# A two-layer decoder trunk on one core: own slots for half of the value weights, the gate scaled into SBUF, a pad 64 bytes wider

## The chip, the cores and the metric

The kernel runs on one core of a Trainium2 chip. What counts is the device time of one execution in microseconds (us), lower being better; the time of a kernel is the median of its runs. A core has five engines that work side by side and each run their own list of instructions in order: TensorE (PE in the profile, its weight loads PEld), VectorE (DVE), ScalarE (ACT), GpSimd (POOL) and SyncE (SP), whose work here is to issue DMA transfers. SBUF is the working memory; PSUM holds the results of TensorE. Semaphores order the engines among each other.

## The reference

1024 tokens of width 1024 pass two residual layers and a last RMS norm. Layer 1 is a gated linear recurrence, layer 2 is attention with a forget gate:

```python
def fox_mixer(h, w_in, b_f, w_out):
    u = h @ w_in
    q, k, v, gate = ...            # 16 heads of 64 each, from the columns of u
    f_logit = u[..., 4 * FOX_WIDTH:] + b_f
    cum = jnp.cumsum(jax.nn.log_sigmoid(f_logit), axis=1)
    logits = (q . k) * scale + (cum_q - cum_k)      # causal
    p = jax.nn.softmax(logits, axis=-1)
    y = (p @ v) * jax.nn.silu(gate)
    return y @ w_out

for i in range(2):
    x = x + (lru_mixer, fox_mixer)[i](rms_norm(x, norm_g[i]), ...)
return rms_norm(x, final_g)
```

All inputs and the output are float32.

## The kernel before

**Products.** A float32 product is made of three matmuls in a faster format: both factors are split into a high part (the value rounded to that format) and a low part (the rest), and high x high, low x high and high x low are added up in PSUM. The activations' parts are called `hh` and `hl`, those of weights `wh` and `wl`. A weight pack of 128x512 numbers is split in three steps by `split_weights`: a DMA brings it into a buffer `wf` (three buffers in all), ScalarE casts it to `wh`, and VectorE (GpSimd in some places) subtracts to get `wl`. The `wh` and `wl` of all weights of layer 2 (query, key, gate, value, output) share four slots each in the pool `wpool`.

**Layer 1** takes the first 440 us or so, layer 2 the rest. The change concerns layer 2, but for the pad.

**Layer 2.** Heads go in pairs. For each head and each half of its 512 queries, `maxima` makes the logits `S` (TensorE), their maximum (VectorE, L702) and the exponentials `p` (ScalarE, L707), 128 queries at a time; `weigh` turns `p` by transposes into PSUM (`pt`), splits it into `ph` and `pl` (ScalarE and VectorE) and multiplies with the values (`O`). In between, as filling for TensorE, `kq_units` makes the next pair's queries and keys, `g_units` its gate, both through `project`, and `values` the values of two pairs at a time.

`project` makes, for each half of the tokens, a product of 24 matmuls in one of two PSUM banks of the tag `g`, multiplies it in place by the row `rs1` of reciprocal RMS values (VectorE, L511), and hands it to `use`. For the gate, `use` is tanh on ScalarE from the PSUM bank into `sg` in SBUF (L672), and then on VectorE (tanh + 1) x gate (L673; the operation is a scalar_tensor_tensor, STT for short), which reads `sg` and the PSUM bank. The bank is free after that.

`values(g)` for g = 1 to 3 is taken up in the heads 3, 7 and 11 (at some 620 to 656, 763 to 800 and 908 to 943 us). It has four weight packs (k = 0, 2, 4, 6). The first two are split before the generator's first `yield`, the third and fourth (k = 4 and 6) after it. They take slots of `wpool`: the first two those that the queries' weights leave, the others those that the gate's weights leave. Then come eight tiles `vps` of 24 matmuls of 128x256, in turn in the two banks `g`; each is split into the values `v` by ScalarE and VectorE (L546).

**What sets the order.** The text of the program gives only a first order: `run` takes steps from the generators as a string of digits and dots says. The framework's scheduler then simulates the program and orders each engine's instructions by it, and gives buffers to tiles in the order in which they come free in that simulation. Each engine runs its list in order, so an instruction that waits holds up all behind it on that engine; the DMA issues on SP's queue likewise.

**Placement.** Pools lie on the left or the right side of SBUF. `pad2` lies on the left, ahead of `hT` (the pool of `hh` and `hl`), `w` (`wpool`), and all left-side pools of both layers. On the right side lie, among others, `rs`, the recurrence's temporaries with the `xch`, `xcl`, `wgh` and `wgl` that layer 1's `gate` products read, and in layer 2 the values, the queries and keys, and `rs1`.

Of the kernel before, what the change touches and what calls it, by code (L numbers as in the profile page):

```python
# [11 lines left out]
F32 = mybir.dt.float32  # L12
F32R = mybir.dt.float32r
BF16 = mybir.dt.bfloat16
AF = mybir.ActivationFunctionType
ALU = mybir.AluOpType

P = 128
SEQ = 1024
HALF = 512  # L20
KT = 8
# [12 lines left out]
def f32(ap):  # L34
    return ap.bitcast(F32)
# [3 lines left out]
def trunk(ctx: ExitStack, tc: tile.TileContext, xt, w0, wg, wo0, pc, gn, gf, w1, wv, wf, bf, wo1, out):  # L39
    nc = tc.nc  # L40

    def pool(name, bufs, **kw):
        return tc.tile_pool(name=name, bufs=bufs, **kw)
# [2 lines left out]
    const.tile([P, 32], F32, name="pad0")  # L46
    ctx.enter_context(pool("edge", 1, side="right")).tile([P, 56], F32, name="pad1")
    dram = ctx.enter_context(pool("dram", 1, space=DRAM))
    ctx.enter_context(pool("gap", 1)).tile([P, 24], F32, name="pad2")
    hpool = ctx.enter_context(pool("hT", 16))  # L50
    wpool = ctx.enter_context(pool("w", 4))
    ps = ctx.enter_context(pool("ps", 2, space=PSUM))
# [3 lines left out]
    def matmul(*args, **kw):  # L56
        pe[0] = nc.tensor.matmul(*args, **kw)  # L57
        return pe[0]
# [26 lines left out]
    def to_hi(hi, src, eng, scale=None):  # L85
        if eng is nc.scalar:
            if scale is None:
                nc.scalar.copy(hi, src)  # L88
            else:
                nc.scalar.activation(hi, src, AF.Copy, scale=scale)  # L90
        elif eng is nc.gpsimd:
            nc.gpsimd.tensor_scalar(hi, src, 1.0 if scale is None else scale, 0.0, ALU.mult, ALU.add)
        elif scale is None:
            eng.tensor_copy(hi, src)
        else:
            eng.tensor_scalar(hi, src, scale, None, ALU.mult)

    def to_lo(lo, src, hi, eng):
        return eng.tensor_tensor(lo, src, f32(hi), ALU.subtract)  # L99

    def split_weights(src, shape, hi_eng, lo_eng, parts=wpool):
        n = shape[0] * shape[1]
        room = -(-n // 64) * 64
        a = wpool.tile([P, room], F32, tag="wf", name="wf", bufs=3)[:, :n]
        b = parts.tile([P, room], F32R, tag="wh", name="wh")[:, :n]
        c = parts.tile([P, room], F32R, tag="wl", name="wl")[:, :n]
        wt, hi, lo = (t.rearrange("p (a b) -> p a b", a=shape[0]) for t in (a, b, c))
        for part, sl in src:
            nc.sync.dma_start(wt[:, :, sl], part)
        to_hi(b, a, hi_eng)  # L110
        to_lo(c, a, b, lo_eng)
        return [(hi[:, k], lo[:, k]) for k in range(shape[0])]
# [66 lines left out]
    late = ctx.enter_context(ExitStack())  # L179
    with ExitStack() as l0:  # L180
# [42 lines left out]
        k = 0  # L223
# [84 lines left out]
        def silu(s, gps, parts=(slice(0, SEQ),)):  # L308
            gs = gps.rearrange("p a b -> p (a b)")
            sg = s["sg"] = long("sg")  # L310
            for cs in parts:
                g_, s_ = gs[:, cs], sg[:, cs]
                nc.vector.tensor_tensor(g_, g_, rs[:, cs], ALU.mult)
                nc.scalar.activation(s_, g_, AF.Tanh, scale=0.5)
                nc.vector.scalar_tensor_tensor(s_, s_, 1.0, g_, ALU.add, ALU.mult)
                yield
# [22 lines left out]
        def outputs(n, parts=(slice(0, SEQ),), gate=itertools.repeat(None)):  # L339
            s = state.pop(n)  # L340
            y = tuple(ypool.tile([P, SEQ], F32R, tag=z, name=z) for z in ("yh", "yl"))
            for cs, _ in zip(parts, gate):
                a_ = s["a"][:, cs]
                nc.vector.tensor_tensor(a_, a_, s["sg"][:, cs], ALU.mult)
                yh, yl = (z[:, cs] for z in y)
                to_hi(yh, a_, nc.scalar)
                to_lo(yl, a_, yh, nc.vector)
            ys.append(y)
# [86 lines left out]
        recur(NB - 1, halves)  # L435
        outputs(NB - 1, halves, silu(state[NB - 1], gps, halves))
        lru.close()
        vpool = late.enter_context(pool("v", 1, side="right"))
        kqpool = late.enter_context(pool("kq", 1, side="right"))
        rpool = late.enter_context(pool("R", 2, side="right"))  # L440
# [4 lines left out]
        rs1 = [rpool.tile([P, HALF], F32, tag="R", name="rs1") for h in range(2)]  # L445
# [9 lines left out]
        for h, cs in enumerate(halves):  # L455
            y = [tuple(z[:, cs] for z in p) for p in ys[-2:]]
            hT[h] = [pair() for k in range(KT)]
            parts = split_x(h, 1)
# [29 lines left out]
    with ExitStack() as l1:  # L488
        tu = l1.enter_context(pool("tu", 1))
        at = l1.enter_context(pool("at", 2))  # L490
# [15 lines left out]
        def project(w, use, hs=(0, 1)):  # L506

            for h in hs:
                pt = ps.tile([P, HALF], F32, tag="g", name="gps1")
                yield from gemm_steps(pt, zip(w, hT[h]))  # L510
                nc.vector.tensor_tensor(pt, pt, rs1[h], ALU.mult)  # L511
                use(h, pt)

        def values(g):

            ex = HEADS if g == 0 else 0
            parts = []
            for k in range(0, KT, 2):
                src = [(wv[g, :, k : k + 2], slice(0, 256))]
                if ex:  # L520
                    src.append((wf[:, k : k + 2], slice(256, 256 + ex)))
                parts += split_weights(src, (2, 256 + ex), nc.scalar, nc.gpsimd if ex else nc.vector)
                if k == 2:
                    yield
            Vs[2 * g], Vs[2 * g + 1] = [], []
            for st in range(8):
                if ex and st % 2:
                    pt = ps.tile([P, SEQ], F32, tag="S", name="vps")[:, : 256 + ex]
                else:
                    pt = ps.tile([P, 256 + ex], F32, tag="g", name="vps")  # L530
                c = (st % 4) * P
                for k in range(KT):
                    xh, xl = hT[st // 4][k]
                    wh, wl = parts[k]
                    xh, xl = xh[:, c : c + P], xl[:, c : c + P]
                    matmul(pt, xh, wh, start=k == 0, stop=False)
                    matmul(pt, xl, wh, start=False, stop=False)
                    matmul(pt, xh, wl, start=False, stop=k == KT - 1)
                    if k % 4 == 1:
                        yield  # L540
                r_ = rms1[st // 4][:, st % 4 : st % 4 + 1]
                for a in range(2):
                    v = vpool.tile([P, 4, HD], F32R, tag=f"v{st}", name=f"v{st}", bufs=2)
                    src = pt[:, a * P : (a + 1) * P].rearrange("p (b d) -> p b d", b=2)
                    to_hi(v[:, 0::3], src, nc.scalar, scale=r_)
                    nc.vector.scalar_tensor_tensor(v[:, 1:3], src, r_, f32(v[:, 0::3]), ALU.mult, ALU.subtract)  # L546
                    Vs[2 * g + a].append(v)
                if ex:
                    nc.vector.tensor_scalar(fz[:, st], pt[:, 256:], r_, None, ALU.mult)
# [10 lines left out]
        def low(pair):  # L560
            return nc.vector if pair else nc.gpsimd

        def kq_units(pair, parts=((1, (0, 1)), (0, (0, 1)))):

            for is_k, hs in parts:
                if hs[0] == 0:
                    kq[pair, is_k] = tuple(
                        kqpool.tile([P, SEQ], F32R, tag=f"qk{p}{is_k}", name=f"qk{p}") for p in "hl"
                    )
                if hs[0] == 0 or pair == 0:  # L570
                    kqw[is_k] = list(weights(w1[is_k * 8 + pair], lo_eng=low(pair)))
                hi, lo = kq[pair, is_k]
                eng = nc.vector if pair == 0 else nc.scalar

                def use(h, pt):
                    cs = halves[h]
                    if is_k:
                        to_hi(hi[:, cs], pt, eng)
                        to_lo(lo[:, cs], pt, hi[:, cs], nc.vector)
                    else:  # L580
                        to_hi(hi[:, cs], pt, eng, scale=0.125)
                        nc.vector.scalar_tensor_tensor(lo[:, cs], pt, 0.125, f32(hi[:, cs]), ALU.mult, ALU.subtract)  # L582

                yield from project(kqw[is_k], use, hs)
# [78 lines left out]
        def g_units(pair, hs=(0, 1)):  # L663

            if hs[0] == 0:
                sgs[pair] = at.tile([P, SEQ], F32, tag="sg", name="sg1")
                gw[0] = list(weights(w1[16 + pair], lo_eng=low(pair)))
            sg = sgs[pair]

            def use(h, pt):  # L670
                g_ = sg[:, h * HALF : (h + 1) * HALF]
                nc.scalar.activation(g_, pt, AF.Tanh, scale=0.5)  # L672
                nc.vector.scalar_tensor_tensor(g_, g_, 1.0, pt, ALU.add, ALU.mult)  # L673

            yield from project(gw[0], use, hs)

# [294 lines left out]
        for hd in range(HEADS):  # L971
# [29 lines left out]
            side = late() if hd == 14 else iter(())  # L1001
# [99 lines left out]
```

## Time and profile before

| | |
|---|---|
| runs | 1130.3, 1131.4 and 1128.25 us, median 1130.3 |
| the profiled execution | 1132.74 us |
| its span, first to last instruction | 1130.9 us, so 1.8 us lie around it |
| mean granted clock of TensorE | 0.995 |
| busy in the span | TensorE 98%, VectorE 67%, ScalarE 52%, GpSimd 15% |
| moved by DMA | 105.43 MB, mean 93 GB/s |

Rows of a timeline give the start in us from the span's start, the duration in us, the engine, the line of the kernel, the operation and its operands (output<-inputs by the program's names, buffer numbers left out), the shapes, and in brackets how long the engine sat idle before, and for what. In grouped rows stand the count, the busy time in us, the mean in ns of one, and the idle time before them. Matmuls are pipelined, so the pace of TensorE is read from one start to the next, not from durations.

### The profile page before, as it was taken

Reading aid. Unit: us, or ns where it says so; the run is one execution under the profiler, and the core shown is the slowest. Engines: PE = TensorE matmul, PEld = TensorE weight load, DVE = VectorE, ACT = ScalarE, POOL = GpSimd, SP = SyncE. Lnnn points to the kernel's source line nnn. Section 1 sums busy time; section 2 is a strip of 40 time slices with the busy share of each in tenths; the row PEclk is TensorE's granted clock in tenths of the full one; section 3 lists DMA queues with packets and bytes.
Section 4 is the critical chain, followed back from the end, with each engine's and each line's share of the span. In section 5 each row is a group of like instructions: output and inputs, shape, how many; then the busy total and the mean of one; then the engine's idle time right before and its main releaser. Section 6 shows DMA issues by size and latency. Waiting matters only on the chain.

```text
span 1130.9 us, 15754 instructions
## 1 busy us (share of the span) xinstructions
PE 1112.0 (98%) x5681; PEld 937.3 (83%) x5681; DVE 762.2 (67%) x1271; ACT 589.6 (52%) x1077; POOL 165.6 (15%) x105
## 2 busy tenths in 40 slices
PE   9999999999999999999999999999999999999997
PEld 7786888888888887988888888888888888878886
DVE  7789756876568789666676466763666645676645
ACT  8387445354453666455555355553555534554435
POOL 1312112121121202330110100101001010010110
PEclk9999999999999999999999999999999999999999
DMA  6111121111211114443334124252142421665445
GB/s 216 52 42 52 43 61 38 52 52 42 61 37 52 56 57 144 124 123 103 99 89 119 52 84 109 75 123 62 58 120 85 110 81 52 182 180 157 151 149 186
DMA packets 63702, 105.43 MB, mean 93 GB/s; under 512 B 9508, under 2 KB 24484, under 8 KB 63624
## 3 DMA queue, kind: packets, MB, share of 16 engines
q1 hardware_dynamic: 63624, 104.42, 31.3%
q8 instruction: 45, 0.74, 0.3%
q14 instruction: 33, 0.27, 0.1%
HBM read 63.30 MB, written 15.93 MB: 70 GB/s over the span
## 4 chain that ended last, share of the span: by engine, by line
PE 87%; DVE 4%; ACT 2%; DMA 2%; issue 2%; POOL 1%; SPq 0%; POOLq 0%; ACTq 0%
PE gps L57 32%; PE ops L57 15%; PE ups L57 10%; PE vps L57 7%; PE S L57 6%; PE O L57 6%; PE pt L61 5%; PE turn L57 3%; PE gate L57 2%; POOL wl L99 1%; DMA wf<-in_w 1%; DVE sq L167 1%; ACT wh L88 1%; DVE x L470 0%; DMA x<-in_xt 0%
## 5 line engine op out<-in xcount | busy, mean ns | idle before, releaser
L57 PE MATMUL gps<-hh,wh 128*128 128x512 f32 x576 | 228.6, 397 | 1.0 <-DVE qkl L582 1.0
L57 PE MATMUL gps<-hl,wh 128*128 128x512 f32 x576 | 226.0, 392 | 0.0
L57 PE MATMUL gps<-hh,wl 128*128 128x512 f32 x576 | 226.0, 392 | 0.0
L88 ACT CAST wh<-wf 128x512 fp32r<-128x512 f32 (+2 forms) x156 | 94.6, 607 | 146.6 <-PE gps L57 49.2
L707 ACT ACTIVATE p<-S,m 128x128 f32<-128x128 f32 (+7 forms) x128 | 94.9, 741 | 135.2 <-DVE m L702 134.1
L99 POOL TENSOR_TENSOR wl<-wf,wh 128x512 fp32r<-128x512 f32 (+1 forms) x60 | 100.7, 1685 | 389.4 <-ACT wh L88 332.5
L99 DVE TENSOR_TENSOR pl<-pt,ph 128x512 fp32r<-128x512 f32 (+1 forms) x198 | 98.8, 540 | 81.7 <-ACT ph L88 81.3
L57 PEld LDWEIGHTS gps<-hl,wh 128*128 128x128 f32 x576 | 108.4, 188 | 23.8
L57 PEld LDWEIGHTS gps<-hh,wh 128*128 128x128 f32 x576 | 108.6, 189 | 20.2 <-DVE qkl L582 1.2
L57 PEld LDWEIGHTS gps<-hh,wl 128*128 128x128 f32 x576 | 108.9, 189 | 19.7 <-POOL wl L99 0.7
L702 DVE CUSTOM_DVE_ANT_0 S<-S,mask 128x128 f32<-128x128 f32 (+7 forms) x128 | 97.3, 761 | 30.2 <-PE S L57 25.8
L734 POOL TENSOR_TENSOR sg<-sg,recb 64x1024 f32<-64x1024 f32 (+1 forms) x17 | 38.8, 2282 | 460.8 <-DMA recb<-recd 400.8
L88 ACT CAST ph<-pt 128x512 fp32r<-128x512 f32 (+1 forms) x198 | 83.6, 473 | 30.6 <-PE pt L61 25.3
L57 PE MATMUL S<-T,U 96*128 96x512 f32 (+7 forms) x384 | 91.7, 348 | 2.4 <-ACT p L707 2.4
L99 DVE TENSOR_TENSOR wl<-wf,wh 128x512 fp32r<-128x512 f32 x96 | 70.0, 733 | 26.5 <-ACT wh L88 25.8
L369 DVE TENSOR_TENSOR x<-x,ops 128x512 f32<-128x512 f32 x80 | 54.1, 682 | 48.1 <-PE ops L57 48.1
L57 PEld LDWEIGHTS S<-T,U 128*128 128x128 f32 (+1 forms) x384 | 68.3, 189 | 15.6 <-ACT p L707 3.6
L61 PE MATMUL pt<-ident,p 128*128 128x128 f32 x576 | 79.4, 273 | 0.0
L57 PE MATMUL ups<-hh,wh 128*128 128x512 f32 x192 | 76.6, 400 | 1.7 <-ACT hh L90 1.0
L61 PEld LDWEIGHTS pt<-ident,p 128*128 128x128 f32 x576 | 67.4, 141 | 12.4 <-issue 2.2
L57 PE MATMUL vps<-wh,hh 128*128 128x256 f32 (+1 forms) x256 | 74.6, 292 | 3.0 <-DVE sg L673 2.1
L57 PE MATMUL ups<-hh,wl 128*128 128x512 f32 x192 | 76.0, 396 | 1.5 <-POOL wl L99 1.5
(176 smaller groups left out, 2260.0 us busy)
## 6 DMA issues: line engine op xcount, KB each, us to landing
wf<-in_w SPq DMA_DIRECT2D x100, 256.0 KB
wf<-in_wo SPq DMA_DIRECT2D x64, 128.0 KB
U<-qkh SPq DMA_DIRECT2D x64, 128.0 KB
T<-qkh SPq DMA_DIRECT2D x28, 256.0 KB
x<-in_xt SPq DMA_DIRECT2D x16, 256.0 KB
x1d<-x SPq DMA_DIRECT2D x16, 256.0 KB
wf<-in_wv SPq DMA_DIRECT2D x16, 256.0 KB
U<-qkl SPq DMA_DIRECT2D x32, 128.0 KB
```

The costliest lines, as they stand in the source:

```text
L57: pe[0] = nc.tensor.matmul(*args, **kw)
L61: pe[0] = nc.tensor.transpose(*args)
L88: nc.scalar.copy(hi, src)
L99: return eng.tensor_tensor(lo, src, f32(hi), ALU.subtract)
L167: eng.tensor_tensor(parts[0], parts[0], sq, ALU.add)
L369: nc.vector.tensor_tensor(x, x, pt, ALU.add)
L702: nc.vector.tensor_tensor_reduce(S[:, :n], S[:, :n], mask[:, SEQ - n :], -1.0, -NEG, ALU.add, ALU.min, accum_out=m)
L707: seen[0] = nc.scalar.activation(p, S[:, :n], AF.Exp, bias=m, scale=-1.0, accum_out=sums[:, i : i + 1])
L734: nc.gpsimd.tensor_tensor(sg, sg, recs[hd // 2][rows, cs], ALU.mult)
```

## The change

Three things are changed.

1. A new pool `vw` on the right side has two slots each for `wh` and `wl`. The third and fourth weight packs of `values(1)` to `values(3)` take them, and the generator yields only after all four packs are split.
2. The scaling by `rs1` moves from `project` into each `use`. For queries and keys it is the same instruction at the same place. For the gate it now writes to `sg` in SBUF, the tanh reads `sg` and writes a new tile `t1` (in the buffers of the tag `xp`), and the STT works on `t1` and `sg`. The number of instructions is the same.
3. `pad2` is 40 instead of 24 numbers wide, so that everything behind it on the left side moves by 64 bytes, from 192 to 0 modulo 256.

```diff
-    ctx.enter_context(pool("gap", 1)).tile([P, 24], F32, name="pad2")
+    ctx.enter_context(pool("gap", 1)).tile([P, 40], F32, name="pad2")
...
+        vwpool = late.enter_context(pool("vw", 2, side="right"))
         vpool = late.enter_context(pool("v", 1, side="right"))
...
                 pt = ps.tile([P, HALF], F32, tag="g", name="gps1")
                 yield from gemm_steps(pt, zip(w, hT[h]))
-                nc.vector.tensor_tensor(pt, pt, rs1[h], ALU.mult)
                 use(h, pt)
...
-                parts += split_weights(src, (2, 256 + ex), nc.scalar, nc.gpsimd if ex else nc.vector)
-                if k == 2:
+                parts += split_weights(
+                    src, (2, 256 + ex), nc.scalar, nc.gpsimd if ex else nc.vector, wpool if ex or k < 4 else vwpool
+                )
+                if k == (2 if ex else KT - 2):
                     yield
...
                 def use(h, pt):
                     cs = halves[h]
+                    nc.vector.tensor_tensor(pt, pt, rs1[h], ALU.mult)
...
                 g_ = sg[:, h * HALF : (h + 1) * HALF]
-                nc.scalar.activation(g_, pt, AF.Tanh, scale=0.5)
-                nc.vector.scalar_tensor_tensor(g_, g_, 1.0, pt, ALU.add, ALU.mult)
+                nc.vector.tensor_tensor(g_, pt, rs1[h], ALU.mult)
+                t = at.tile([P, HALF], F32, tag="xp", name="t1", bufs=2)
+                nc.scalar.activation(t, g_, AF.Tanh, scale=0.5)
+                nc.vector.scalar_tensor_tensor(g_, t, 1.0, g_, ALU.add, ALU.mult)
```

The scheduler moves instructions at the three `values` stages. The first stage serves as the example. On TensorE, the end of the gate's second half (`gps1`) and the start of the value tiles: before, the first tile's last pack (`wh_5480`) stands behind the gate and the four `O` products, and the second tile begins after it.

```order
L57 MATMUL gps1_5387<-hl_3438,wh_5255 128x512
L57 MATMUL O_5326<-ph_5444,v6_3962 128x256
L57 MATMUL O_5326<-pl_5445,v6_3962 128x256
L57 MATMUL O_5326<-ph_5447,v7_3994 128x128
L57 MATMUL O_5326<-pl_5448,v7_3994 128x128
L57 MATMUL vps_5485<-wh_5480,hh_3295 128x256
L57 MATMUL vps_5485<-wh_5480,hl_3296 128x256
L57 MATMUL vps_5485<-wl_5481,hh_3295 128x256
L57 MATMUL vps_5485<-wh_5480,hh_3297 128x256
L57 MATMUL vps_5485<-wh_5480,hl_3298 128x256
L57 MATMUL vps_5485<-wl_5481,hh_3297 128x256
L57 MATMUL vps_5516<-wh_5307,hh_3283 128x256
```

After the change the second tile (`vps_5525`) follows the `O` products at once:

```order
L57 MATMUL gps1_5407<-hl_3441,wh_5262 128x512
L57 MATMUL O_5345<-ph_5464,v6_3965 128x256
L57 MATMUL O_5345<-pl_5465,v6_3965 128x256
L57 MATMUL O_5345<-ph_5467,v7_3997 128x128
L57 MATMUL O_5345<-pl_5468,v7_3997 128x128
L57 MATMUL vps_5525<-wh_5314,hh_3286 128x256
```

The first tile (`vps_5494`) now ends ahead of the gate's last six matmuls: its last six are done ahead of the transposes `pt_5440` of before (`pt_5460` now).

On VectorE, at the same place, before: the scaling in PSUM, the low part of the fourth pack, the sum of `yo`, the STT of the gate, and then the first value tile.

```order
L99 TENSOR_TENSOR pl_5448<-pt_5440,ph_5447 128x128
L511 TENSOR_TENSOR gps1_5387<-gps1_5387,rs1_3254 128x512
L99 TENSOR_TENSOR wl_5481<-wf_5479,wh_5480 128x512
L780 TENSOR_TENSOR yo_4994<-yo_4994,O_5326 64x512
L673 SCALAR_TENSOR_TENSOR sg1_5247<-sg1_5247,gps1_5387 128x512
L546 SCALAR_TENSOR_TENSOR v0_5510<-vps_5485,rms10_3251,v0_5510 128x128
```

And after, where the two operations on the first value tile stand ahead of the scaling, and the low part is that of the next pair's weights:

```order
L548 SCALAR_TENSOR_TENSOR v0_5519<-vps_5494,rms10_3254,v0_5519 128x128
L99 TENSOR_TENSOR pl_5465<-pt_5460,ph_5464 128x256
L99 TENSOR_TENSOR pl_5468<-pt_5460,ph_5467 128x128
L548 SCALAR_TENSOR_TENSOR v0_5522<-vps_5494,rms10_3254,v0_5522 128x128
L675 TENSOR_TENSOR sg1_5254<-gps1_5407,rs1_3257 128x512
L99 TENSOR_TENSOR wl_5773<-wf_5771,wh_5772 128x512
L785 TENSOR_TENSOR yo_5001<-yo_5001,O_5345 64x512
L678 SCALAR_TENSOR_TENSOR sg1_5254<-t1_5491,sg1_5254 128x512
```

On SP's queue, half a head earlier, the loads of the third and fourth packs. Before, the third (`wf_5473`) stands ahead of the T loads and the fourth (`wf_5479`) behind the U loads:

```order
L109 DMA wf_5473<-in_wv 128x512
L591 DMA T0_3575<-qkh_4854 64x1024
L592 DMA T0_3575<-qkh_4854 64x1024
L593 DMA T0_3575<-qkl_4855 64x1024
L605 DMA U_3577<-cumd_3567 2x512
L602 DMA U_3577<-qkh_5056 64x512
L603 DMA U_3577<-qkh_5056 64x512
L604 DMA U_3577<-qkl_5057 64x512
L109 DMA wf_5479<-in_wv 128x512
```

After, the fourth (`wf_5331`) stands right behind the T loads, and two loads of the next pair's key weights (`in_w1`) take places among the U loads:

```order
L109 DMA wf_5325<-in_wv 128x512
L594 DMA T0_3578<-qkh_4861 64x1024
L595 DMA T0_3578<-qkh_4861 64x1024
L596 DMA T0_3578<-qkl_4862 64x1024
L109 DMA wf_5331<-in_wv 128x512
L608 DMA U_3580<-cumd_3570 2x512
L109 DMA wf_5765<-in_w1 128x512
L605 DMA U_3580<-qkh_5063 64x512
L606 DMA U_3580<-qkh_5063 64x512
L607 DMA U_3580<-qkl_5064 64x512
L109 DMA wf_5771<-in_w1 128x512
```

On ScalarE the casts of the third and fourth packs move from the head's second half into the half before, to places directly ahead of the exponentials `p` of 384 and of 512 columns, and two casts of the next pair's key weights take the places they leave.

## The prediction

> **What bounds the kernel now.** I read the page's first part, the waits of TensorE, the timeline around the longest recurring ones, and then the rows of what they wait for.
>
> ```profile
> PE 1112.0 (98%) x5681; PEld 937.3 (83%) x5681; DVE 762.2 (67%) x1271; ACT 589.6 (52%) x1077; POOL 165.6 (15%) x105
> ```
>
> ```profile
> PE vps L57 <- DVE sg L673: 2.1, 3, 0.7
> ...
> PE vps L57 <- ACT wh L88: 0.9, 3, 0.3
> PE vps L57 <- DVE wl L99: 0.7, 3, 0.2
> ```
>
> TensorE is the bound: it is busy 98% of the span, and of the engines that feed it none passes 67%. Three of its waits belong to `vps` (the value projection), come three times each and are what this change touches (columns: us in all, times, longest). The first of the three stages, on TensorE:
>
> ```profile
> 631.43 0.39 PE L57 MATMUL gps<-hl,wh 128*128 128x512 f32 x1
> ...
> 631.96 0.27 PE L57 MATMUL O<-pl,v 128*128 128x128 f32 x1
> 632.53 0.39 PE L57 MATMUL vps<-wh,hh 128*128 128x256 f32 x1 [0.30 <-ACT wh L88]
> ...
> 633.26 0.39 PE L57 MATMUL vps<-wl,hh 128*128 128x256 f32 x1 [0.22 <-DVE wl L99]
> 633.48 0.28 PE L57 MATMUL vps<-wh,hh 128*128 128x256 f32 x1
> 633.60 0.28 PE L57 MATMUL vps<-wh,hl 128*128 128x256 f32 x1
> ...
> 634.70 0.39 PE L57 MATMUL vps<-wh,hh 128*128 128x256 f32 x1 [0.70 <-DVE sg L673]
> ```
>
> A running `vps` matmul starts 0.12 us after the one before (633.48, 633.60); the first after a wait takes 0.22 (633.26 to 633.48). From 631.96 to 634.70 are 2.74 us; one 128-wide `O` (0.06, half of a 256-wide one) and six `vps` would need 0.78. With the slow start at 634.70 (0.10) the stage loses 2.06 us. Its idle time is 0.30 + 0.22 + 0.70 = 1.22 us. The other two look alike: 1.22 us idle in each stretch from the last `O` to the second tile.
>
> ```profile
> 775.10:777.75 2.65, 1.43 (x9) 1.00 0.13 29
> 777.75:781.30 3.55, 3.55 (x17) 0.54 0.36 131
> 919.80:922.45 2.65, 1.43 (x10) 1.00 0.20 38
> 922.45:926.00 3.55, 3.55 (x29) 1.00 0.32 119
> ```
>
> (Columns: length, TensorE busy and its matmuls, granted clock, DMA share, GB/s.) The rows also show a second price: after the second stall the granted clock is 0.54 for 3.55 us and 17 matmuls run where the third stage runs 29, so 12 x 0.12 = 1.4 us are lost. One stall of three had it.
>
> **Part 1, the splits ahead.** The wait at 632.53 is for the fourth pack's cast, the one at 633.26 for its low part. With slots of their own both are ready before the gate ends, so these waits go; the order shows the fourth pack's matmuls ahead of the gate's last group. What stays is the bank.
>
> **Part 2, the gate.** The second tile needs the PSUM bank of the gate's second half. It is freed today by the second of these:
>
> ```profile
> 631.86 0.70 DVE L511 TENSOR_TENSOR gps<-gps,rs 128x512 f32<-128x512 f32 x1 [0.94 <-PE gps L57]
> ...
> 633.96 0.69 DVE L673 SCALAR_TENSOR_TENSOR sg<-sg,gps 128x512 f32<-128x512 f32 x1
> 634.56 0.34 DVE L546 SCALAR_TENSOR_TENSOR v<-vps,rms,v 128x128 fp32r<-128x128 f32 x1
> ```
>
> Afterwards the first of them, now writing to SBUF, frees it. Its nearest row, PSUM times `rs` into SBUF, has the same length:
>
> ```profile
> L279 DVE TENSOR_TENSOR us<-ups,rs 128x512 f32<-128x512 f32 x4 | 2.7, 688 | 0.9 <-PE ups L57 0.8
> ```
>
> It can start 0.43 us after the start of the last gate matmul (631.43 to 631.86), ends at 632.56, and TensorE follows 0.05 later (the old STT ends at 634.65, the matmul starts at 634.70): 632.61. TensorE could go on at 632.02. So 0.59 + 0.10 for the slow start = 0.69 us stay, and 2.06 - 0.69 = 1.37 us are won, 4.1 us in three stages. The tanh and the STT that follow keep their number and move from PSUM to SBUF operands; none holds a bank any more.
>
> The scaling now stands behind both `v` operations of the first tile on VectorE. That tile ends some 2.5 us before the gate does (three transposes, four `O` and six gate matmuls lie between). Two `v` casts of 0.37 on ScalarE (row 634.04 below), two STT of 0.34 (634.56) and the `ph` and `pl` operations between them (some 0.6) need about 2.0 us, so I count nothing, with 0.7 us to spare; the cover gone it costs one more pair of `v` operations, 0.37 + 0.34, or 0.7 a stage.
>
> **Part 3, loads and casts moved ahead.** The third and fourth casts now stand ahead of two exponentials `p`, and the fourth load behind the T loads:
>
> ```profile
> 590.51 0.36 SPq L109 DMA_DIRECT2D wf<-in_wv  x1
> ...
> 601.95 0.46 SPq L602 DMA_DIRECT2D U<-qkh  x1
> ...
> 654.25 4.39 SPq L109 DMA_DIRECT2D wf<-in_w  x4
> ```
>
> ```profile
> 593.55 0.58 ACT L707 ACTIVATE p<-S,m 128x384 f32<-128x384 f32 x1 [1.89 <-DVE m L702]
> ...
> 597.86 0.69 ACT L707 ACTIVATE p<-S,m 128x512 f32<-128x512 f32 x1 [1.89 <-DVE m L702]
> ...
> 634.04 0.37 ACT L90 ACTIVATE v<-vps,rms 128x128 fp32r<-128x128 f32 x1 [0.34 <-PE vps L57]
> ...
> 656.94 0.62 ACT L88 CAST wh<-wf 128x512 fp32r<-128x512 f32 x1 [0.59 <-DMA wf<-in_w]
> ```
>
> ```profile
> 593.20:596.70 3.50, 3.50 (x21) 2.93 (x20) 1.01 (x4) 1.64 (x4) 0.19 (x1) 1.00 0.87 181
> ```
>
> ```profile
> 599.10 0.62 DVE L99 TENSOR_TENSOR pl<-pt,ph 128x256 fp32r<-128x256 f32 x2 [1.27 <-ACT ph L88]
> ...
> 600.19 0.28 PE L57 MATMUL O<-pl,v 128*128 128x256 f32 x1
> ```
>
> A load takes about 2.7 us (the first issued at 654.25, its cast at 656.94). The third load keeps its place (590.51); its cast (0.62) can run at 593.2 and ends at 593.85, 0.3 behind the start of the first `p`. The fourth load reuses that buffer, so it is issued at about 594.6, while the T loads keep the DMA engines 0.87 busy until 596.7; it lands at 597.2 to 598. Its cast then ends at 597.8 to 598.6, and the `p` of 597.86, queued behind it on ScalarE, is 0 to 0.7 us late. Next behind it are two `ph` casts, whose `pl` run from 599.10 to 599.72, and the first `O` on a `pl` starts at 600.19, when the first of the two has been done for some 0.75 us. That hides most: 0 to 0.3 us a stage, I take 0.1, in all 0.3. Without that cover it is 0.7 a stage. Of SP's queue, the U loads at 601.95 stand behind one moved weight load that waits only for the fourth pack's low part (about 599), so they keep their time. The places that the two casts leave on ScalarE and VectorE are filled by two of the next pair's, as many and as long: nothing.
>
> Another row speaks against the gate's new form:
>
> ```profile
> 624.08 1.29 POOL L789 TENSOR_TENSOR yo<-yo,sg 128x512 f32<-128x512 f32 x1
> ...
> 634.00 1.28 POOL L789 TENSOR_TENSOR yo<-yo,sg 128x512 f32<-128x512 f32 x1 [8.63 <-DVE yo L780]
> ```
>
> ```profile
> 624.27 1.65 DVE L99 TENSOR_TENSOR wl<-wf,wh 128x512 fp32r<-128x512 f32 x1 [1.39 <-ACT wh L88]
> ```
>
> A VectorE operation with two SBUF inputs took 1.65 instead of 0.69 us beside GpSimd's product: it ended 0.55 after that. The gate's STT gets two SBUF inputs, and GpSimd's product at 634.00 starts 0.04 us after it. If it is held up 1.3 us, the `v` operations behind it wait; but they need the second tile, which ends only at 632.6 + 24 x 0.12 = 635.5, so nothing is lost. The Trainium skill ("SBUF — State Buffer", section "Who interferes with whom") calls the port pair that VectorE shares with GpSimd an exclusive lock; the 1.65 us row agrees. By it alone, with no cover, the sum would be 3.9 us worse.
>
> **Part 4, the pad.** It moves all left-side tiles, weights and activations among them, from 192 to 0 modulo 256 bytes. The rows of layer 1's `gate` have such operands already (they lie on the right side):
>
> ```profile
> L57 PE MATMUL gps<-hh,wh 128*128 128x512 f32 x576 | 228.6, 397 | 1.0 <-DVE qkl L582 1.0
> L57 PE MATMUL gps<-hl,wh 128*128 128x512 f32 x576 | 226.0, 392 | 0.0
> ...
> L57 PE MATMUL ups<-hh,wh 128*128 128x512 f32 x192 | 76.6, 400 | 1.7 <-ACT hh L90 1.0 <-DVE us L279 0.4
> L57 PE MATMUL ups<-hl,wh 128*128 128x512 f32 x192 | 76.1, 396 | 0.1
> ...
> L57 PE MATMUL ops<-yh,wh 128*128 128x512 f32 x192 | 75.6, 394 | 1.2 <-ACT yh L88 0.7 <-DVE x L470 0.5
> ...
> L57 PE MATMUL ops<-yl,wh 128*128 128x512 f32 x192 | 73.9, 390 | 0.2 <-DVE yl L99 0.2
> ...
> L57 PE MATMUL gate<-xch,wgh 128*128 128x512 f32 x48 | 18.6, 395 | 0.0
> ...
> L57 PE MATMUL gate<-xcl,wgh 128*128 128x512 f32 x48 | 17.9, 394 | 0.0
> ```
>
> The two `gate` forms average 394.5 ns, `gps` 394.5, `ops` 392, `ups` 398. Over the kernel's some 2,900 matmuls of these three kinds (three forms of 576, 192 and 192) the bounds are +2.5 ns (+7.2 us) and -3.5 ns (-10 us). `gps`, more than half of them, says 0.0, which I take. DMA into these tiles changes its alignment too; no TensorE wait of the three stages names a DMA, so a quicker or slower load counts nothing.
>
> **The sum.** The profiled execution took 1132.7 us, 2.4 above the median of 1130.3, and held one clock dip. From it: 1132.7 - 4.1 - 1.4 + 0.3 = 1127.5. For the median I count half a dip (one stall in three had one here; the 2.4 us suggest that a median run may have none): 1130.3 - 4.1 - 0.7 + 0.3 = **1125.8 us**. The Trainium skill ("TensorE: Matmul & The Clock Gate", section "What's actually happening") gives the half clock to a free-running window of 3.4 us that was idle; the dip's 3.55 us agree, but TensorE was half busy before it. Read strictly, no stage should dip, and the sum would be 1126.5.
>
> **Rivals.**
> (A) Slower: the pad costs matmul pace. Price: 2.5 ns on 2,900 matmuls, 1125.8 + 7.2 = 1133.0; from 1.6 ns (4.5 us) on it eats the gain; the largest difference of two rows, 390 to 394, would give 1137. For: `ops` against `gate`. Against: `gps` and `ups`. Chance 0.12. The reverse, a pace 2 ns quicker, gives 1120: 0.07.
> (B) The fourth cast makes `p` late: 0.7 x 3 instead of 0.3 in all, 1127.6; should the shared port also hold VectorE at a bad moment in each stage, 1129. For: DMA share 0.87 at that load. Against: 1.89 us of slack on ScalarE before that `p`. Chance 0.16.
> (C) The wait is only replaced: the scaling comes late behind the `v` operations, 0.7 x 3, 1127.9. For: the new order on VectorE. Against: the 0.7 us to spare. Chance 0.10.
>
> **The numbers.** The forecast has 0.55, with a range of its own of 1124 to 1127.6. About 0.3% (3.4 us) is what a measurement of this kernel can tell from no change; the bounds are 1126.9 and 1133.7. Faster: 0.45 of the forecast, 0.07 of the quicker pace, 0.05 of the others: 0.57. Slower: 0.06, out of A with a larger price. Same: the rest, 0.37. The range of 8 in 10 takes in B, C and most of A: 1121.5 to 1132.
>
> **What would show it.** Right: in the waits of TensorE, `vps` on `wh` and `wl` are gone and one `vps` wait of about 0.5 us a stage, on the scaling (L675), is left; no clock below 1.00 behind the stages. Wrong: new `S` or `O` waits near 598 to 600 us, a `vps` wait with a scaling that starts over 0.5 us behind the gate, or the mean of `gps` off 394 ns by over 1.5 ns with no new wait at all.

## The result, and the profile after

The changed kernel takes 1124.5 us (median of 6 runs, 1122.3 to 1125.7) beside 1130.1 us before (6 runs): a ratio of 0.9955, 95% interval 0.9938 to 0.9972. A second comparison gave 0.9959 (0.9944 to 0.9974). The forecast was 1125.8. The total came out near it, but three of its terms did not.

The page of the changed kernel, its first line, and the one wait of TensorE between 560 and 960 us, where the three stages lie (columns: us in all, times, longest):

```profile
PE 1106.5 (98%) x5681; PEld 933.0 (83%) x5681; DVE 764.6 (68%) x1271; ACT 589.3 (52%) x1077; POOL 166.5 (15%) x105
```

```profile
PE O L57 <- DVE pl L99: 0.7, 3, 0.2
```

There is no wait of `vps` at all any more: those on `wh` and `wl` are gone, as forecast, and the one on the bank is gone too, which was not. In their place stands a wait that was not there before, three times: `O` on `pl`.

The first stage on TensorE, from the gate's last matmul on:

```profile
630.79 0.40 PE L57 MATMUL gps<-hl,wh 128*128 128x512 f32 x1
...
631.32 0.27 PE L57 MATMUL O<-pl,v 128*128 128x128 f32 x1
631.42 0.33 PE L57 MATMUL vps<-wh,hh 128*128 128x256 f32 x1
631.60 0.28 PE L57 MATMUL vps<-wh,hl 128*128 128x256 f32 x1
```

And VectorE and GpSimd at the same place:

```profile
630.18 0.34 DVE L548 SCALAR_TENSOR_TENSOR v<-vps,rms,v 128x128 fp32r<-128x128 f32 x1
631.22 0.69 DVE L675 TENSOR_TENSOR sg<-gps,rs 128x512 f32<-128x512 f32 x1 [0.70 <-PE gps L57]
...
633.32 0.69 DVE L678 SCALAR_TENSOR_TENSOR sg<-t,sg 128x512 f32<-128x512 f32 x1
```

```profile
633.37 1.80 POOL L794 TENSOR_TENSOR yo<-yo,sg 128x512 f32<-128x512 f32 x1 [9.60 <-DVE yo L785]
```

The second value tile starts at 631.42, while the scaling that frees the gate's bank runs from 631.22 to 631.91. So the second tile is not in the gate's bank. It is in the first tile's own, which the second `v` operation had left at 630.52. The scaling did start 0.43 us behind the last gate matmul and last 0.69 us, as counted, and the `v` operations ahead of it were done in time; only, nothing waits for it.

The same stretches as before, TensorE alone (length, busy and matmuls, clock, DMA share, GB/s). The first row is the first stage, the other four belong to the second and third:

```profile
631.42:634.05 2.63, 2.63 (x24) 1.00 0.12 43
773.45:776.10 2.65, 2.65 (x24) 1.00 0.18 49
776.10:779.65 3.55, 3.55 (x32) 1.00 0.30 116
915.35:918.00 2.65, 2.65 (x24) 1.00 0.14 26
918.00:921.55 3.55, 3.55 (x32) 1.00 0.34 129
```

Where 8 to 10 matmuls ran in 2.65 us, 24 run now, and the clock behind the second stage is 1.00. Each stage has won the whole 2.06 us.

The loss lies half a head earlier. ScalarE, SP and TensorE there:

```profile
592.20 0.62 ACT L88 CAST wh<-wf 128x512 fp32r<-128x512 f32 x1 [3.01 <-DMA wf<-in_wv]
592.73 0.57 ACT L712 ACTIVATE p<-S,m 128x384 f32<-128x384 f32 x1
...
596.57 0.62 ACT L88 CAST wh<-wf 128x512 fp32r<-128x512 f32 x1 [2.32 <-DMA wf<-in_wv]
597.09 0.68 ACT L712 ACTIVATE p<-S,m 128x512 f32<-128x512 f32 x1
```

```profile
588.02 0.36 SPq L109 DMA_DIRECT2D wf<-in_wv  x1
...
593.57 0.33 SPq L109 DMA_DIRECT2D wf<-in_wv  x1
```

```profile
592.94 0.39 PE L57 MATMUL O<-pl,v 128*128 128x512 f32 x1
593.44 0.73 PE L57 MATMUL S<-T,U 128*128 128x512 f32 x2
...
598.18 0.39 PE L57 MATMUL O<-ph,v 128*128 128x256 f32 x1
598.80 0.38 PE L57 MATMUL O<-pl,v 128*128 128x256 f32 x1 [0.24 <-DVE pl L99]
```

(The T and U loads bring the tiles that the logits `S` are made of.) ScalarE sits 3.0 and 2.3 us on the two loads, with an exponential queued behind each. The third pack's load took 4.2 us to its cast (588.02 to 592.20), the fourth's 3.0. The first exponential's maximum was ready at 591.04 (VectorE's row ends there), so it ran 1.7 us late, the second 1.0 us. On TensorE the `S` at 593.44 comes 0.27 us later than at the pace of before, and 598.80 follows 598.18 by 0.62 instead of 0.12. Compared at equal places of the program (the `O` at 589.87 before and 587.39 after, the `S` at 600.47 and 599.20), the lead of the changed kernel shrinks from 2.48 to 1.27 us; behind the stage it is 3.33 (the `S` at 654.96 and 651.63), so the stage itself did win 2.06. With the other two stages it is some 1.1 us a stage, on average, that is given back.

### The profile page after: what moved, and what is told of

Its sections match the earlier page's. It is cut to its first block, busy times and chain, and to the rows that moved or that the text cites. A ratio compares the mean times of both kernels' runs of the same rounds, so it can differ in the third digit from the quotient of the medians.

```text
span 1123.4 us, 15748 instructions
## 1 busy us (share of the span) xinstructions
PE 1106.5 (98%) x5681; PEld 933.0 (83%) x5681; DVE 764.6 (68%) x1271; ACT 589.3 (52%) x1077; POOL 166.5 (15%) x105
## 5 line engine op out<-in xcount | busy, mean ns | idle before, releaser
L57 PE MATMUL gps<-hh,wh 128*128 128x512 f32 x576 | 227.9, 396 | 1.4 <-DVE qkl L585 1.4
L99 POOL TENSOR_TENSOR wl<-wf,wh 128x512 fp32r<-128x512 f32 (+1 forms) x60 | 98.1, 1641 | 388.5 <-ACT wh L88 337.4
L57 PE MATMUL ops<-yh,wh 128*128 128x512 f32 x192 | 75.4, 393 | 1.2 <-ACT yh L88 0.6
L57 PE MATMUL ups<-hl,wh 128*128 128x512 f32 x192 | 76.1, 396 | 0.3 <-DVE hl L242 0.2
```

## The experiments

Twelve runs follow; 10 and 11 repeat the changed kernel and run 4. Where a ratio is given, it is against the kernel before on the same chip, with its 95% interval. Two theories opened the study. A: the stages won 2.06 us each and lost 1.1 each to the early casts, and the pad is worth nothing. B: about 2 us that this does not explain come from the pad.

**1. The pad alone**

```diff
-    ctx.enter_context(pool("gap", 1)).tile([P, 24], F32, name="pad2")
+    ctx.enter_context(pool("gap", 1)).tile([P, 40], F32, name="pad2")
```

> The kernel before with pad2 40 wide and nothing else. Theory A (the pad is worth nothing; all of the 5.5 us comes from the three value stages and the clock behind them): 1130 us, within 0.1% of before, the mean of gps at 393 to 394 ns as before. Theory B (the alignment of the weights and activations gives the some 2 us that the stages do not explain): 1128 us, and the gps, ups or ops rows 0.5 to 1 ns shorter. Theory C (it costs pace, rival A of the prediction): 1133.

Measured: 1127.7 us against 1129.0, ratio 0.9989 (0.9980 to 0.9998). A small gain, the upper end just short of none. The sum's zero for the pad was wrong; the trace shows where. Layer 1 has the same order of matmuls in all kernels, so one can take the time from its 600th to its 1800th matmul. Before, then the changed kernel, then the pad alone (each its own trace):

```profile
149.03:421.93 272.90, 272.90 (x1202) 1.00 0.16 50
```

```profile
147.15:419.15 272.00, 272.00 (x1201) 1.00 0.16 50
```

```profile
146.82:418.82 272.00, 272.00 (x1202) 1.00 0.16 50
```

272.00 instead of 272.90 us, with TensorE busy throughout and the clock at 1.00: the same 1200 matmuls run 0.75 ns faster each, on average. Taken apart by product, from one start to the next, `gate` went from 230.2 to 226.7 ns, `ups` from 227.9, `ops` from 227.0 and `gps` from 226.8 to the same 226.7. The other kernels with the pad at 40 (runs 3, 4, 10 and 11) show 272.00 as well, and those with 24 (runs 2, 5 and 12) 272.90. So this part is no accident of an execution.

**2. The changed kernel without the pad**

```diff
-    ctx.enter_context(pool("gap", 1)).tile([P, 40], F32, name="pad2")
+    ctx.enter_context(pool("gap", 1)).tile([P, 24], F32, name="pad2")
```

> The changed kernel with pad2 back at 24. Theory A: 1124.5 us, as the change. Theory B: 1126.5, 2 us above it. Theory C: under 1122.

Measured: 1126.3 us, ratio 0.9984 (0.9972 to 0.9995), as theory B had it. The stretch of layer 1 has the slow time:

```profile
147.08:419.98 272.90, 272.90 (x1201) 1.00 0.16 50
```

**3. The changed kernel with the gate as before**

```diff
-                nc.vector.tensor_tensor(g_, pt, rs1[h], ALU.mult)
-                t = at.tile([P, HALF], F32, tag="xp", name="t1", bufs=2)
-                nc.scalar.activation(t, g_, AF.Tanh, scale=0.5)
-                nc.vector.scalar_tensor_tensor(g_, t, 1.0, g_, ALU.add, ALU.mult)
+                nc.vector.tensor_tensor(pt, pt, rs1[h], ALU.mult)
+                nc.scalar.activation(g_, pt, AF.Tanh, scale=0.5)
+                nc.vector.scalar_tensor_tensor(g_, g_, 1.0, pt, ALU.add, ALU.mult)
```

> The changed kernel with the gate as before (scaled in PSUM, tanh and the last product from PSUM), own slots and pad kept. Theory A (the trace after shows the second value tile starting before the scaling ends, so it does not use the gate's bank; the splits alone give the whole 2.06 us a stage): 1124.5 us and no vps wait on sg. Theory D (the prediction's: the second tile needs the gate's bank, and the gate in SBUF shortens that wait): a vps wait of 0.7 to 1.4 us a stage comes back, 1126.6 to 1128.6.

Measured: 1123.3 us, ratio 0.9964 (0.9951 to 0.9976), no different from the changed kernel's 0.9955 and 0.9959, and no `vps` wait in the trace. Theory D, the prediction's, falls: beside the splits the gate's new form is worth nothing.

**4. The casts held back**

The casts of the third and fourth packs may be ordered only after the exponentials of 128 and of 256 columns of the next head's first half (`seen[0]` is the exponential that the text issued last). Slots, gate and pad are those of the changed kernel. The fourth load comes later too: at 603.60 us in run 11's trace, where the changed kernel has it at 593.57.

```diff
-    def split_weights(src, shape, hi_eng, lo_eng, parts=wpool):
+    def split_weights(src, shape, hi_eng, lo_eng, parts=wpool, after=ExitStack):
...
-        to_hi(b, a, hi_eng)
+        with after():
+            to_hi(b, a, hi_eng)
...
-                    src, (2, 256 + ex), nc.scalar, nc.gpsimd if ex else nc.vector, wpool if ex or k < 4 else vwpool
+                    src, (2, 256 + ex), nc.scalar, nc.gpsimd if ex else nc.vector, wpool if ex or k < 4 else vwpool,
+                    ExitStack if ex or k < 4 else lambda: tc.issue_after(seen[0].ins),
                 )
-                if k == (2 if ex else KT - 2):
+                if k == 2 or (k > 2 and not ex):
                     yield
...
                 next(vals)
+                side = itertools.islice(vals, 2)
```

> The changed kernel, with the casts of the third and fourth packs held back until after the exponentials of 128 and of 256 columns of the next head's first half, so that none stands ahead of an exponential while its load is under way. Theory A (these two casts cost 1.1 us a stage in the trace after, as an S and an O wait): 1124.5 - 3.3 = 1121.2 us, and the O waits on pl are gone. Theory E (that cost comes from something else, or moves on with the casts): 1124 to 1125.

Measured: 1123.0 us, ratio 0.9957 (0.9941 to 0.9974). The `O` waits on `pl` are gone, but the ratio is that of the changed kernel. Its executions had a mean granted clock of 0.9972, those of the changed kernel 0.9982. Over the 124 executions of all kernels, each kernel with a level of its own, the time rises by 0.80 us (standard error 0.06) for each 0.001 that the clock is lower. At equal clock this kernel came out some 2 us below the changed one. Run 11 repeats it beside run 10.

**5. The gate alone**

The kernel before with the new gate and the scaling moved into each `use` as in the change; pad 24 and no own slots.

```diff
...
                 g_ = sg[:, h * HALF : (h + 1) * HALF]
-                nc.scalar.activation(g_, pt, AF.Tanh, scale=0.5)
-                nc.vector.scalar_tensor_tensor(g_, g_, 1.0, pt, ALU.add, ALU.mult)
+                nc.vector.tensor_tensor(g_, pt, rs1[h], ALU.mult)
+                t = at.tile([P, HALF], F32, tag="xp", name="t1", bufs=2)
+                nc.scalar.activation(t, g_, AF.Tanh, scale=0.5)
+                nc.vector.scalar_tensor_tensor(g_, t, 1.0, g_, ALU.add, ALU.mult)
```

> The kernel before with only the gate scaled into SBUF (pad 24, no own slots). In this kernel the first value tile is still unfinished when the gate ends, so the second tile does need the gate's bank. Theory A (the gate's new form is worth something only there): the waits on sg and on wl go, that on wh (0.57 us a stage with its slow start) stays, since the scheduler puts the second tile into the wait on wl; 1.4 us a stage are won, 4.2 in all, without the early casts: ratio to before 0.9963. Theory D (the prediction's price for the bank): the wait on sg is replaced by one of 0.6 us on the scaling: ratio 0.998 at best. Theory F (the gate's new form is worth nothing anywhere, as in the run with the old gate): 1.000.

Measured: 1129.6 us, ratio 1.0006 (0.9994 to 1.0019): nothing, as theory F said. But the waits are not those of before. On TensorE, in all, times, longest:

```profile
PE vps L57 <- DVE v L545: 3.7, 3, 1.2
...
PE vps L57 <- ACT wh L88: 0.9, 3, 0.3
```

And in the first stage:

```profile
629.65 0.39 PE L57 MATMUL vps<-wh,hh 128*128 128x256 f32 x1 [0.30 <-ACT wh L88]
629.87 0.28 PE L57 MATMUL vps<-wh,hl 128*128 128x256 f32 x1
...
633.22 0.28 PE L57 MATMUL vps<-wl,hh 128*128 128x256 f32 x1
634.74 0.36 PE L57 MATMUL vps<-wh,hh 128*128 128x256 f32 x1 [1.25 <-DVE v L545]
```

The waits on `wl` and on the gate did go, as theory A expected. The second tile starts two matmuls after the first tile's last pack came, and both tiles are then finished together at 633.2. Now the third tile needs a bank, both are still to be emptied by the `v` operations, and TensorE waits 1.25 us for them. The wait has moved by one tile and is no shorter: 1.25 us of idle time, where 0.22 and 0.70 us stood before.

**6, 7, 8, 9. Where the pad's part comes from**

Four times the changed kernel with other paddings, each executed once. `pad2` lies ahead of `hT`, an added `pad3` between `hT` (activations) and the pools behind it (weights among them).

```diff
# 6: hT at 192, the pools behind at 0 (modulo 256 bytes)
+    ctx.enter_context(pool("gap", 1)).tile([P, 24], F32, name="pad2")
     hpool = ctx.enter_context(pool("hT", 16))
+    ctx.enter_context(pool("gap3", 1)).tile([P, 16], F32, name="pad3")
# 7: hT at 0, the pools behind at 192
+    ctx.enter_context(pool("gap", 1)).tile([P, 40], F32, name="pad2")
     hpool = ctx.enter_context(pool("hT", 16))
+    ctx.enter_context(pool("gap3", 1)).tile([P, 48], F32, name="pad3")
# 8: all at 128
+    ctx.enter_context(pool("gap", 1)).tile([P, 72], F32, name="pad2")
# 9: hT at 0, the pools behind at 128
+    ctx.enter_context(pool("gap", 1)).tile([P, 40], F32, name="pad2")
     hpool = ctx.enter_context(pool("hT", 16))
+    ctx.enter_context(pool("gap3", 1)).tile([P, 32], F32, name="pad3")
```

> The changed kernel with pad2 at 24 and 16 numbers more behind hT, so that hT (hh, hl) stays at 192 modulo 256 and all pools behind it (weights, x, y, layer 2's tiles) are at 0. In the traces so far 1100 matmuls of layer 1 take 0.84 us less with the pad at 40, the same in four kernels to the nanosecond scale. If the activations' alignment is the cause, this look has the slow pace; if it is that of the pools behind, the quick one.

> The reverse: pad2 at 40 and 48 numbers more behind hT, so that hT is at 0 and all pools behind it are at 192 modulo 256. If the activations' alignment is the cause, the quick pace of layer 1; if that of the pools behind, the slow one (0.84 us more over the 1100 matmuls).

> The changed kernel with pad2 at 72: all left-side tiles at 128 modulo 256. If 0 modulo 256 is what counts, the slow pace of 24; if any place but 192 is as good, the quick one of 40.

> The changed kernel with 32 numbers more behind hT: hT at 0, all pools behind it at 128 modulo 256. Theory G (what counts for TensorE's pace is the distance between the activations and the weights, which was a multiple of 256 in all quick kernels so far): a slow layer 1 as in the two runs with a distance of 64 and 192, 2.4 to 4.9 us more over the matmuls 600 to 1800 than the changed kernel. Theory H (only odd multiples of 64 are bad): the pace of the changed kernel or of the pad at 24.

The stretch of layer 1 in the four, in this order, each from its own trace:

```profile
144.63:422.42 277.79, 277.79 (x1201) 1.00 0.16 49
```

```profile
146.68:422.47 275.79, 275.79 (x1201) 1.00 0.16 49
```

```profile
145.34:417.88 272.54, 272.54 (x1201) 1.00 0.16 50
```

```profile
145.25:423.07 277.82, 277.82 (x1202) 1.00 0.16 49
```

The times of the single executions were 1130.6, 1128.8, 1123.6 and 1132.7 us. Neither the activations' place nor that of the pools behind it is what counts by itself: with `hT` at 192 and the rest at 0, or at 0 and the rest at 192, layer 1 is 2.9 to 4.9 us slower than in any kernel that moves both together. The forecast of theory G came true, and H fell with run 9: at a distance of 64, 128 or 192 modulo 256 between `hT` and the pools behind it the pace is lost, at a distance of 0 it is kept. What remains between 24, 72 and 40 (272.90, 272.54, 272.00) may be the place of both against the right side of SBUF, which did not move; no run tests that alone.

Taken apart by product, the distance is not the whole of it. In run 6 `gps` and `ups`, which read `hT` and the weights, went from 226.7 to 233.2 and 233.3 ns. But `ops`, whose two operands both lie behind `hT` and kept their distance, went to 228.9, and `gate`, whose operands lie on the right side and moved in none of these kernels, to 229.2. In run 7 all four took 229 to 231 ns. What in the chip makes this so, these runs do not show.

**10 and 11. The changed kernel and the held-back casts, side by side**

The same kernels as the change and run 4.

> The changed kernel once more, beside the next one on the same chip. 0.9955 to 0.9965 of before.

> The kernel with the two casts held back, once more. Theory A (3.3 us of the changed kernel's loss is gone, and what hid it in the first comparison was the granted clock, 0.997 on average against 0.998): 0.993 to 0.995 of before, 1 to 3 us under the changed kernel. Theory E (the gain moves on to another wait): as the changed kernel.

Measured: 1124.9 us, ratio 0.9959 (0.9944 to 0.9974), and 1122.2 us, ratio 0.9936 (0.9920 to 0.9952), with mean clocks of 0.9976 and 0.9980. Theory A holds in the main: holding the casts back gives 2.6 us more on the medians, 2.3 at equal clock (1124.3 and 1122.0 at 0.998, standard errors 0.4 each), of the 3.3 that it named. ScalarE where it sat on the loads, in run 11:

```profile
589.95 0.58 ACT L714 ACTIVATE p<-S,m 128x384 f32<-128x384 f32 x1 [1.89 <-DVE m L709]
...
594.23 0.69 ACT L714 ACTIVATE p<-S,m 128x512 f32<-128x512 f32 x1 [1.89 <-DVE m L709]
```

The exponentials wait for their maxima again, 1.89 us as before the change, and TensorE:

```profile
596.47 0.28 PE L57 MATMUL O<-ph,v 128*128 128x256 f32 x1
596.58 0.27 PE L57 MATMUL O<-pl,v 128*128 128x256 f32 x1
```

This kernel is faster than the kernel before and than the change, and the best one found here.

**12. The splits alone**

The kernel before with own slots and all four splits ahead, the gate in PSUM and the pad at 24.

```diff
+        vwpool = late.enter_context(pool("vw", 2, side="right"))
...
+                    src, (2, 256 + ex), nc.scalar, nc.gpsimd if ex else nc.vector, wpool if ex or k < 4 else vwpool
+                )
-                if k == 2:
+                if k == (2 if ex else KT - 2):
```

> The kernel before with only the own slots and the splits ahead (gate in PSUM as before, pad 24). Theory A: 3 x 2.06 us won and 3 x 1.1 lost, about 3 us: 0.997 of before, no vps wait in the waits of TensorE. Theory D: vps waits on sg remain, 0.999.

Measured: 1125.3 us, ratio 0.9963 (0.9949 to 0.9976), and no `vps` wait. VectorE in the first stage:

```profile
628.66 0.34 DVE L548 SCALAR_TENSOR_TENSOR v<-vps,rms,v 128x128 fp32r<-128x128 f32 x1
629.70 0.70 DVE L675 TENSOR_TENSOR gps<-gps,rs 128x512 f32<-128x512 f32 x1 [0.69 <-PE gps L57]
...
631.80 0.69 DVE L677 SCALAR_TENSOR_TENSOR sg<-sg,gps 128x512 f32<-128x512 f32 x1
```

The old gate frees its bank at 632.49. The second tile started at 629.90 and needs 24 x 0.12 = 2.9 us, so the third, which takes that bank, comes at 632.8: the old gate is done 0.3 us ahead of need.

Put together at a mean clock of 0.998 (standard errors 0.2 to 0.5 us):

| kernel | us | against before |
|---|---|---|
| before (51 runs) | 1128.6 | |
| gate alone | 1129.1 | +0.5 |
| pad alone | 1126.8 | -1.8 |
| splits and gate, pad 24 | 1126.0 | -2.6 |
| splits alone | 1125.4 | -3.2 |
| splits and pad, old gate | 1124.3 | -4.3 |
| the change | 1124.4 and 1124.3 | -4.3 |
| the change, casts held back | 1122.3 and 1122.0 | -6.5 |

The splits give 2.6 to 3.2 us, the pad 1.1 to 1.8, the gate nothing (0 to 0.6 us lost).

## Why the prediction was right, and where it was not

**The stall and its first two waits.** The 2.06 us a stage, read from starts, stood. The waits on `wh` and `wl` went as forecast.

**The bank: the step that failed.** The prediction said "The second tile needs the PSUM bank of the gate's second half", and left 0.69 us a stage for it. That was so before, where the first tile was unfinished when the gate ended. With the splits ahead the first tile is finished 2.5 us before the gate ends, its two `v` operations empty its bank during the gate's last matmuls, and the second tile takes that bank. The order quoted ahead of the prediction showed the first tile ahead of the gate's last six matmuls and both `v` operations ahead of the scaling; that its bank would be free was there to be read. It left 3 x 0.69 = 2.1 us of gain uncounted. The prediction's own signs say as much: the `vps` wait on the scaling that was to be left did not come, and a new `O` wait near 598 us, named as a sign of being wrong, did.

**The gate.** It follows that the part of the gain that the prediction gave to the gate's new form was the splits' own. Alone it moves the wait by one tile (run 5), and beside the splits it saves nothing (run 3), since the gate's bank is needed only 2.9 us later.

**The casts ahead: mis-sized.** The term was 0.1 us a stage, with a bound of 0.7; it measured some 1.1 (and 2.3 us in all came back when the casts were held). The mechanism was rival B's, but it began one exponential earlier. The load's 2.7 us came from a place where two more weight loads, but no T load, were issued close behind it. Here three T loads were issued within 1.7 us behind the third pack's load, and it took 4.2 us to its cast. That they slowed it is likely, but no run tests it alone. So already the first exponential was 1.7 us late, where 0.3 was counted, and the second 1.0.

**The pad: mis-sized.** The term was 0, from the means of `gate` and `gps`, with bounds of -10 and +7 us. It measured -1.2 us (ratio 0.9989), of which 0.9 us are seen in 1200 matmuls of layer 1. The comparison failed twice. The means are of modelled durations, which hide the pace: from start to start, `gate` took 230.2 ns in the stretch of layer 1 before the change and `gps` 226.8, where the means gave both 394.5. And `gate` was taken as the picture of tiles at 0 modulo 256, yet it is the row that gained most a matmul from the pad, with operands that the pad does not move. That `gps` would gain nothing was nearly right (0.2 ns); `ups` and `gate` gained. In layer 2 the pace of `gps` is 230.3 ns before and after the change.

**The clock: mis-sized.** Half a dip, 0.7 us, was counted, since the profiled execution "held one clock dip". Its trace has three, each of 3.41 us at half clock, from 10.0, 105.6 and 778.0 us on, and only the last lies behind a value stage (first row; the 3.55 us of the prediction was the length of its stretch). Run 1 has the same three `vps` waits at that stage and no dip behind them (second row):

```profile
778.02:781.43 3.41, 3.41 (x18) 0.50 0.32 114
```

```profile
773.00:779.00 6.00, 5.30 (x44) 1.00 0.27 90
```

So a dip is not a fixed price of the stall, and what the change saves of dips has to be read from many executions. The mean clock of the runs of before is 0.9976, of the changed kernel 0.9979; by 0.80 us per 0.001 that is some 0.2 us, less than these clocks, given to 0.001, can tell.

So -4.1 - 0.7 + 0.3 became about -6.2 (stages) + 3 (casts) - 1.2 (pad) - 0.2 (clock) = -4.6 us, beside the -5.1 and -4.6 us of the two ratios. Errors of 2 and 3 us of opposite sign made the total right; that it came so near is luck. Of the rivals, B came true beside the forecast, A did not (the pad helps), and C did not: the scaling was in time.

**The shared port.** The STT with two SBUF inputs started 0.05 us ahead of GpSimd's product (633.32 and 633.37), and this time GpSimd was held: 1.80 us instead of 1.28. VectorE kept its 0.69, and TensorE lost nothing, as argued. The Trainium skill ("SBUF — State Buffer", section "Who interferes with whom") has it that the order of issue decides who blocks; the two rows of before and of after, with opposite orders, agree.

## What to carry to other kernels

When a wait goes, work out what the next user of the resource will be in the new order, and not in the old: here the second tile changed banks, and the part of the change that was to free the old bank became idle. A cast moved ahead of a chain of exponentials holds them up until its load has landed, so count what the load takes at that place, beside the transfers that run there; hold it back by an anchor in the order, which here gave half as much again as the change itself. A gain below 0.3% is read from the same stretch of the same instructions in two traces, where it stands to the hundredth of a microsecond, while medians move with the granted clock.

## What the runs showed of the hardware that was not expected

The pace of a stream of matmuls depends on where the SBUF tiles lie. The same 1200 matmuls took 272.0 us with the activations and the weights a multiple of 256 bytes apart and both at 0 modulo 256, 272.5 and 272.9 us with both at 128 and at 192, and 275.8 to 277.8 us with the two pools 64, 128 or 192 bytes off each other, always at a granted clock of 1.00 and, for kernels with the same layout, equal to 0.01 us. The Trainium skill ("SBUF — State Buffer", section "Who interferes with whom") says that TensorE waits for no other engine at SBUF. If that holds, no other engine's reading is the cause. The place of a matmul's own two operands is not the whole cause either: those of `gate` never moved, and it took 226.7 to 230.7 ns. The cause stays open.

The granted clock dipped in other places from run to run: in the stretch around 105 us of the traces here it was below 1.00 in some and at 1.00 in others of kernels with the same layer 1. In the 3.41 us ahead of the three dips of the kernel before, TensorE was busy for 2.19, 1.71 and 2.18 us, so a stretch need not be idle to be followed by half clock. Each 0.001 of mean clock went with 0.80 us.
